# A two-layer decoder trunk: the order of loads and casts in the first pass, and the second mixer's outputs on quarters of the array

## The chip, the cores and the metric

The kernel runs on one core of a Trainium2 chip. Its time is the device time of one execution in microseconds (us). Of the kernel before there are three timed runs, with a median of 755.52 us (754.93 to 756.13), and one profiled execution. PE is the matrix engine, DVE the vector engine, ACT the scalar engine, POOL the GpSimd engine and SP the engine that issues most of the DMAs.

## What is computed

The input is `x`, 256 tokens of width 1024, and one conditioning vector `c`. Each of two layers does

```
mod = silu(c) @ w_ada[i] + b_ada[i]          # six vectors: shift, scale, gate, twice
h = rmsnorm(x, norm_mix[i]) * (1 + sc1) + sh1
x = x + g1 * mixer(h)                        # layer 0: dilated attention; layer 1: gated linear attention
h = rmsnorm(x, norm_ffn[i]) * (1 + sc2) + sh2
x = x + g2 * conv_ffn(h)
```

and the output is `rmsnorm(x, norm_final)`. The second mixer, the gated linear attention, works on chunks of 64 tokens: within a chunk the output is `A @ v` with a masked 64x64 matrix `A` (the part called intra here), and from the chunks before comes `q_t @ s_prev`, with a state of 128x256 per head (the part called inter). Each of its four heads has 128 key and 256 value columns. Its output is normalized per head, multiplied by a gate and projected.

## The kernel before

Activations lie transposed, features on the 128 partitions and the 256 tokens along the free axis, in eight tiles `kt` of 128 features. Most products are done as three passes in the fp32r format: a weight is cast to a high part `whi` by ACT, DVE subtracts that from the weight to get the low part `wlo`, and PE adds hi x hi, hi x lo and lo x hi. The second mixer's products within the chunks are plain fp32 matmuls, each of which shows as two instructions in the trace.

**First pass.** Lines 415 to 470 prepare the eight tiles of the first attention projections. For each `kt`, SP loads one chunk of the modulation weights (1024 KB, called `ada_raw` or `early_x` by the room it lands in) and one chunk of the projection weights (960 KB, `raw`); up to tile 3 each is loaded in two pieces. DVE forms two dot products of the modulation chunk with `silu(c)` (L161), first that of the scale and then that of the shift; ACT adds the bias to each (`mod`, L170 and L172); DVE scales x (`xr`, L432); ACT adds the shift and rounds (`hhi`, L436); DVE makes `hlo` (L440). Beside that ACT casts the weights in two pieces (L448, 768 and 1152 columns) and DVE makes their low parts (L453). The order on ACT is written out by hand: scale's `mod`, first cast, shift's `mod`, `hhi`, second cast; on DVE: two dots, `xr`, first low part, `hlo`, second low part. PE runs the products of a tile (L684 to L690) in a hand-set order, and every tile starts with hi x hi.

Raw weights share four buffers (`raw`), so SP can issue a load only when the DVE has made the low part of an older one, and the odd modulation chunks share one room (`early_x`), free when the dots of the odd tile before are done. SP issues in one queue; where a load's room isn't free, the scheduler may have put a later load ahead of it. Behind the last load SP writes the table of attention biases to DRAM (`rows_d`), from which POOL's own DMA queue fetches the shifted bias tiles (L384 and L385, 16 small transfers for the first two pairs of heads). Behind these POOL loads two more modulation chunks (L495) into the rooms of `early_x` and `x_all`.

**After the first pass.** ACT and DVE take the products out of the PSUM banks (`evacuate`, L597 to L605), which makes room for the next projection, `raw_queries` (L654); the weights of that and of the next values go through the same `raw` buffers, and their casts (L191) are on ACT too.

**Second mixer.** `in_turn` puts groups of products of PE one behind the other. `masked` transposes the decayed keys, forms `A` and copies its causal half into a zeroed tile `a_t` of 128x(2x128) per head, which holds two chunks on its diagonal; `states` forms the states; `outputs` adds the intra part (L1169: 8 matmuls of 128x128 with 128 columns for two heads) and the inter part (L1177: 24 matmuls onto 64 of the output rows with 64 columns) in one PSUM bank for each head; ACT squares each bank, DVE adds, PE sums over features (L1200), and DVE multiplies by the inverse norm (L1210). `key_weights` casts and splits the key and query weights of a head; `decayed` applies the decays (L1104 to L1106).

Of the kernel before, what the change touches and what calls it, by code (L numbers as in the profile page):

```python
# [14 lines left out]
U32 = mybir.dt.uint32  # L15
AF = mybir.ActivationFunctionType
# [41 lines left out]
def trunk(ctx: ExitStack, tc: tile.TileContext, I, out):  # L58
# [37 lines left out]
    def col(at):  # L96
        return small[:, at : at + 1]
# [311 lines left out]

    rooms = [z.rearrange("p k t -> p (k t)")[:, 0:2048] for z in (early_all, x_all)]  # L410

    def load(kt):
        chunk = rooms[0] if kt % 2 else wraw.tile([P, 2048], F32, tag="raw", name="ada_raw")
        for c in (slice(D, 2 * D), slice(0, D)) if kt < 4 else (slice(0, 2 * D),):
            nc.sync.dma_start(chunk[:, c], I["w_ada"][0, kt][:, c])
        raw = wraw.tile([P, 2048], F32, tag="raw", name="raw")
        for c in pieces if kt < 4 else (slice(0, 15 * P),):
            last_load[0] = nc.sync.dma_start(raw[:, c], I["w0"][kt][:, c])
        raw0.append(raw)
        w0.append([wspl.tile([P, 2048], F32R, tag=f"w{part}", name=f"w{part}") for part in ("hi", "lo")])  # L420
        return chunk

    def dots(kt, between=None):
        chunk = load(kt)
# [20 lines left out]
    def cast(kt, half):  # L445
        c = pieces[half]
        with behind(on_act[0]):
            on_act[0] = nc.scalar.copy(w0[kt][0][:, c], raw0[kt][:, c])  # L448
# [4 lines left out]
            on_dve[0] = nc.vector.tensor_tensor(w0[kt][1][:, c], raw0[kt][:, c], w0[kt][0][:, c].bitcast(F32), op=ALU.subtract)  # L453

    def tile_of(kt):
        def first_cast(last):
            on_act[0] = last
            cast(kt, 0)
            return on_act[:1]

        dots(kt, first_cast)
        scaled(kt)
        shifted(kt)
        cast(kt, 1)

    for kt in range(KT):
        tile_of(kt)
# [8 lines left out]
            low(kt, 1)  # L476
    scale_terms(1)
    with tc.issue_after(last_load[0].ins):
        nc.sync.dma_start(rows_d, rows)
        nc.sync.dma_start(small[:, C_CW:], I["small"][:, C_CW:])  # L480

    o_hi, o_lo = [], []
# [219 lines left out]
    for kt in range(1, KT):  # L702
# [4 lines left out]
        for part in (1, 2):  # L707
# [235 lines left out]
    def gt(shape, name, dt=F32, bufs=1, tag=None):  # L943
        return gla.tile(shape, dt, tag=tag or name, name=name, bufs=bufs)
# [125 lines left out]
        with behind(*(run if run[0] else ())):  # L1070
            run[0] = products()

    def key_weights(hd):
        after = ([last_nz], [last_log], last_e)[hd] if hd < 3 else ()
        return split(I["w_qk_b"][hd][:, KT * P :] if hd == 0 else I["w_qk_b"][hd], KT * P if hd == 0 else 2048, after=(after, after))

    def keyed(hd, w, between=None):
        pqk = bank("pqk", "ttpp"[hd])
# [18 lines left out]
    def decayed(hd, pq, pk):  # L1097
        part = min(hd, 1)
        e_q, e_k, e_d, dec = gates[part]
        c = slice(T * (hd - PARTS[part][0]), T * (hd - PARTS[part][0]) + T)  # L1100
        q_t = gt([P, T], "q_t", bufs=4)
        keys = gt([P, 2 * T], "keys", bufs=2)
        k_t, k_d = keys[:, :T], keys[:, T:]
        nc.vector.tensor_tensor(k_d, pk, e_d[:, c], op=ALU.mult)  # L1104
        nc.vector.tensor_tensor(k_t, pk, e_k[:, c], op=ALU.mult)
        nc.vector.scalar_tensor_tensor(q_t, pq, P ** -0.5, e_q[:, c], op0=ALU.mult, op1=ALU.mult)  # L1106
        return q_t, k_t, k_d

    last_st, kv_copy = [None], [None]

    sides = [slice(CH * odd, CH * odd + CH) for odd in range(2)]

    def masked(tag, *two):
        turned, pa = bank("kdt", tag), bank("a", tag)
        kd = gt([P, 2 * T], "kdT", bufs=2)
        a_t = [gt([P, 2, P], "a_t", bufs=4) for _ in two]
        halves = [(i, t, slice(T * i + P * t, T * i + P * t + P)) for i in range(2) for t in range(2)]
        for to in a_t:
            nc.gpsimd.memset(to, 0.0)

        def products():
            for i, t, c in halves:
                last = nc.tensor.transpose(turned[:, c], two[i][2][:, P * t : P * t + P], ident)
            for i, t, c in halves:
                for to in sides:
                    own, at = (slice(z + to.start, z + to.stop) for z in (P * t, c.start))
                    with behind(last):
                        last = mm(pa[to, at], two[i][1][:, own], two[i][0][:, own], start=True, stop=True)
            return last

        in_turn(products)
        nc.scalar.copy(kd, turned)
        for i in range(2):
            for to in sides:
                from_pa = pa[to, T * i : T * i + T].rearrange("p (a b) -> p a b", a=2)[:, :, to]
                nc.vector.copy_predicated(a_t[i][to, :, to], causal[to, :, to].bitcast(U32), from_pa)
        return kd, a_t

    def states(first, kd):
        kv = [bank("kv", tag) for tag in ("s", "s", "t" if first else "s")]  # L1140

        def products():
            for i, n in ((0, 0), (0, 1), (1, 0), (1, 1), (0, 2), (1, 2)):
                t, r = n // 2, slice(CH * (n % 2), CH * (n % 2) + CH)
                last = mm(kv[n][:, T * i : T * i + T], kd[r, T * i + P * t : T * i + P * t + P],
                              v[t][r, T * (first + i) : T * (first + i) + T], start=True, stop=True)
            return last

        in_turn(products)
        st = [gt([P, 2 * T], f"st{n}") for n in range(3)]  # L1150
        kv_copy[0] = nc.scalar.copy(st[0], kv[0])
        for n in (1, 2):
            for i in range(2):
                part = min(first + i, 1)
                at = 4 * (first + i - PARTS[part][0]) + n
                c = slice(T * i, T * i + T)
                last_st[0] = nc.vector.scalar_tensor_tensor(st[n][:, c], st[n - 1][:, c], gates[part][3][:, at : at + 1], kv[n][:, c],
                                                            op0=ALU.mult, op1=ALU.add)
        return st

    def outputs(first, two, a_t, st):
        po = [bank("o", "s") for _ in range(2)]

        def products():
            for i in range(2):
                for et in range(2):
                    ev = slice(T * (first + i) + P * et, T * (first + i) + P * et + P)
                    for t in range(2):
                        mm(po[i][:, T * et + P * t : T * et + P * t + P], v[t][:, ev], a_t[i][:, t, :],  # L1169
                           start=(et == t == 0), stop=False)  # L1170
            for i in range(2):
                for et in range(2):
                    for n in range(1, 4):
                        c = slice(CH * n, CH * n + CH)
                        for to in sides:
                            at = T * i + P * et + to.start
                            last = mm(po[i][to, T * et + CH * n : T * et + CH * n + CH], st[n - 1][:, at : at + CH], two[i][0][:, c],  # L1177
                                      start=False, stop=(et == 1 and n == 3))
            return last

        in_turn(products)
        sq = gt([P, 4 * T], "osq", tag="D1").rearrange("p (i e t) -> p i e t", i=2, e=2)
        for i in range(2):
            nc.scalar.activation(sq[:, i, :, :], po[i].rearrange("p (e t) -> p e t", e=2), AF.Square)
        acc = gt([P, 2 * T], "oacc", tag="keys", bufs=2).rearrange("p (i t) -> p i t", i=2)
        nc.vector.tensor_tensor(acc, sq[:, :, 0, :], sq[:, :, 1, :], op=ALU.add)
        return po, acc

    o_n = []
# [1 line left out]
    def normed_outputs(first, po, acc):  # L1191
# [15 lines left out]
        for i in range(2):  # L1207
            on = gt([P, 2 * T], "on", tag=f"st{i}" if first else f"on{i}").rearrange("p (e t) -> p e t", e=2)
            for et in range(2):
                last_on = nc.vector.scalar_tensor_tensor(on[:, et, :], po[i][:, T * et : T * et + T], col(C_GN + et), rr[:, T * i : T * i + T],  # L1210
                                               op0=ALU.mult, op1=ALU.mult)
            o_n.append(on)
        return last_on

    r_g = []
# [278 lines left out]
```

## Time and profile before

| what | value |
|---|---|
| median of three runs | 755.52 us |
| the profiled execution, its own time | 754.74 us |
| its span | 753.0 us |
| PE busy | 745.0 us |
| DVE busy | 630.5 us |
| ACT busy | 491.5 us |
| DMA moved | 186.83 MB, mean 248 GB/s |
| granted PE clock | 1.0 |

The span is what the profile covers; the execution's own time is 1.74 us longer. A line number (L453) is that of the kernel before. Times in the rows below are us from the start of the span. "Idle before" an instruction is time in which its engine had nothing to do, and the arrow names what ended it. A row with x4 stands for four merged instructions.

### The profile page before, as it was taken

What the parts mean: (1) busy time and instruction counts of PE and PEld (TensorE: products, weight loads), DVE (VectorE), ACT (ScalarE), POOL (GpSimd) and SP (SyncE); (2) the same over time, 40 slices, a digit from 0 to 9 for tenths busy, and PEclk for the clock granted to TensorE, in tenths of its full rate; (3) what the DMA queues carried; (4) which work ended last, traced back from release to release, by engine and by line L of the source; (5) the groups of instructions that cost most, each with busy time, mean ns of one, the idle gap of its engine ahead of it and who ended that gap; (6) DMA issues with size and microseconds to landing.
All of it is one profiled execution on the core that took longest, in us unless ns stands there. A gap on an engine that the chain in (4) does not pass through costs nothing.

```text
span 753.0 us, 16106 instructions
## 1 busy us (share of the span) xinstructions
PE 745.0 (99%) x6474; PEld 723.7 (96%) x6474; DVE 630.5 (84%) x1124; ACT 491.5 (65%) x954; POOL 78.2 (10%) x148
## 2 busy tenths in 40 slices
PE   9999999999999999999999999999999999999997
PEld 7999999999999999999999998899999999999996
DVE  7988977887978688999988778987897989898672
ACT  6467676576666588676766547845878766666552
POOL 6243320320200010000000002000010000000100
PEclk9999999999999999999999999999999999999999
DMA  8999788888886666866646985873475755556741
GB/s 340 417 353 369 246 297 308 292 280 280 288 282 227 235 224 220 285 225 229 241 147 229 329 315 180 340 277 130 155 279 172 277 188 204 198 181 216 266 149 56
DMA packets 31997, 186.83 MB, mean 248 GB/s; under 512 B 4386, under 2 KB 4770, under 8 KB 16051
## 3 DMA queue, kind: packets, MB, share of 16 engines
q1 hardware_dynamic: 26816, 162.38, 60.0%
q0 software_dynamic: 4784, 23.09, 9.4%
q8 instruction: 50, 0.82, 0.4%
q10 hardware_dynamic: 322, 0.35, 0.1%
q14 instruction: 25, 0.20, 0.1%
HBM read 184.70 MB, written 1.10 MB: 247 GB/s over the span
## 4 chain that ended last, share of the span: by engine, by line
PE 88%; DVE 5%; DMA 3%; ACT 2%; issue 1%; SPq 0%; ACTq 0%; DVEq 0%
PE pab L216 10%; PE pab L217 10%; PE pab L218 10%; PE pd L216 5%; PE pd L217 5%; PE pd L218 5%; PE pqk L216 5%; PE pqk L217 4%; PE pqk L218 4%; PE pv L217 3%; PE pv L218 3%; PE pv L216 3%; DMA early_x<-in_w_ada 2%; PE py L217 2%; PE py L218 2%; PE py L216 2%
## 5 line engine op out<-in xcount | busy, mean ns | idle before, releaser
L195 DVE TENSOR_TENSOR wlo<-raw,whi 128x1024 fp32r<-128x1024 f32 (+3 forms) x254 | 272.4, 1105 | 54.7 <-ACT whi L191 53.6
L191 ACT CAST whi<-raw 128x1024 fp32r<-128x1024 f32 (+3 forms) x254 | 228.6, 949 | 107.4 <-PE pab L217 40.8
L218 PE MATMUL pab<-hhi,wlo 128*128 128x256 f32 x672 | 184.9, 276 | 0.0
L217 PE MATMUL pab<-hlo,whi 128*128 128x256 f32 x672 | 184.8, 277 | 0.0
L216 PE MATMUL pab<-hhi,whi 128*128 128x256 f32 x672 | 183.4, 277 | 0.0
L218 PEld LDWEIGHTS pab<-hhi,wlo 128*128 128x128 f32 x672 | 126.2, 188 | 0.0
L217 PEld LDWEIGHTS pab<-hlo,whi 128*128 128x128 f32 x672 | 126.0, 188 | 0.2
L216 PEld LDWEIGHTS pab<-hhi,whi 128*128 128x128 f32 x672 | 125.2, 188 | 0.1
L217 PE MATMUL pd<-glo,whi 128*128 128x256 f32 x352 | 97.1, 276 | 0.0
L218 PE MATMUL pd<-ghi,wlo 128*128 128x256 f32 x352 | 97.1, 276 | 0.0
L216 PE MATMUL pd<-ghi,whi 128*128 128x256 f32 x352 | 96.8, 276 | 0.0
L216 PE MATMUL pqk<-hhi,whi 128*128 128x256 f32 x314 | 88.2, 281 | 0.0
L217 PE MATMUL pqk<-hlo,whi 128*128 128x256 f32 x314 | 87.0, 277 | 0.0
L218 PE MATMUL pqk<-hhi,wlo 128*128 128x256 f32 x314 | 87.0, 277 | 0.0
L161 DVE CUSTOM_DVE_ANT_0 ada_raw<-ada_raw,c_bc 128x1024 f32<-128x1024 f32 x52 | 61.4, 1222 | 8.2 <-DMA ada_raw<-in_w_ada 8.2
L217 PEld LDWEIGHTS pd<-glo,whi 128*128 128x128 f32 x352 | 66.1, 188 | 0.0
L218 PEld LDWEIGHTS pd<-ghi,wlo 128*128 128x128 f32 x352 | 66.1, 188 | 0.0
L216 PEld LDWEIGHTS pd<-ghi,whi 128*128 128x128 f32 x352 | 65.9, 188 | 0.0
L216 PEld LDWEIGHTS pqk<-hhi,whi 128*128 128x128 f32 x314 | 59.1, 188 | 0.5
L217 PEld LDWEIGHTS pqk<-hlo,whi 128*128 128x128 f32 x314 | 59.0, 188 | 0.0
L218 PEld LDWEIGHTS pqk<-hhi,wlo 128*128 128x128 f32 x314 | 59.0, 188 | 0.0
L897 ACT ACTIVATE r<-pab,small 128x256 f32<-128x256 f32 x86 | 46.8, 561 | 15.7 <-DVE r L900 15.6
(244 smaller groups left out, 1500.8 us busy)
## 6 DMA issues: line engine op xcount, KB each, us to landing
raw<-in_w_up SPq DMA_DIRECT2D x42, 1024.0 KB, 4.8
ada_raw<-in_w_ada SPq DMA_DIRECT2D x24, 1024.0 KB, 5.0
raw<-in_w_down SPq DMA_DIRECT2D x32, 704.0 KB, 5.1
raw<-in_wqk SPq DMA_DIRECT2D x18, 1024.0 KB, 5.8
raw<-in_wv SPq DMA_DIRECT2D x14, 768.0 KB, 6.3
early_x<-in_w_ada POOLq DMA_DIRECT2D x9, 1024.0 KB, 6.6
x_all<-in_w_ada POOLq DMA_DIRECT2D x9, 1024.0 KB, 6.2
raw<-in_w_out_a SPq DMA_DIRECT2D x4, 1024.0 KB, 5.3
```

The source lines that it names most:

```text
L161: last_dot[0] = nc.vector.tensor_tensor_reduce(w, w, c_bc, op0=ALU.mult, op1=ALU.add, scale=1.0, scalar=0.0, accum_out=dot,)
L191: copied[0] = nc.scalar.copy(hi[:, c], raw[:, c])
L195: last_lo[0] = nc.vector.tensor_tensor(lo[:, c], raw[:, c], hi[:, c].bitcast(F32), op=ALU.subtract)
L216: mm(ps, a[0], b[0], start=start, stop=False)
L217: mm(ps, a[0], b[1], start=False, stop=False)
L218: return mm(ps, a[1], b[0], start=False, stop=stop)
L897: nc.scalar.activation(r, u[:, :T], AF.Identity, scale=cw[2], bias=col(C_CB + 44 * l + f))
```

## The change

In the first pass every load is queued on SP behind the one before it, in the order modulation chunk, projection chunk, tile by tile, and the write of `rows_d` goes behind the loads of tile 5 and not behind all loads. From tile 3 on, the first cast stands ahead of both `mod`s on ACT and the second cast between them, so both stand ahead of `hhi`. The casts of the first weights after the pass are queued behind the last `hhi` (`after=on_act`).

In the second mixer, the low parts of the last head's key weights are queued on DVE behind `q_t` of the second head. `a_t` loses its empty halves. The intra part becomes 32 matmuls of 64x64 with 64 columns: the first and second chunk of a token half lie on the upper and lower 64 partitions and go to two PSUM banks, so that a bank now holds the even or odd chunks of both heads, and no longer all chunks of one head. The inter part has its 24 matmuls as before, to the new places. The squares and the normalization read the banks in the new order, 64 columns at a time; two heads' states 0 and 1 share one tile, as do two heads' outputs.

```diff
+    def in_turn(to, of):
+        with behind(*(last_load if last_load[0] else ())):
+            last_load[0] = nc.sync.dma_start(to, of)
     def load(kt):
...
-            nc.sync.dma_start(chunk[:, c], I["w_ada"][0, kt][:, c])
+            in_turn(chunk[:, c], I["w_ada"][0, kt][:, c])
...
-            last_load[0] = nc.sync.dma_start(raw[:, c], I["w0"][kt][:, c])
+            in_turn(raw[:, c], I["w0"][kt][:, c])
+        if kt == 5:
+            in_turn(rows_d, rows)
...
     def tile_of(kt):
-        def first_cast(last):
+        def one_cast(last):
             on_act[0] = last
+            cast(kt, int(kt > 2))
+            return on_act[:1]
+
+        chunk = load(kt)
+        if kt > 2:
             cast(kt, 0)
-            return on_act[:1]
-
-        dots(kt, first_cast)
+        dots(kt, chunk, one_cast)
         scaled(kt)
         shifted(kt)
-        cast(kt, 1)
+        if kt < 3:
+            cast(kt, 1)
...
     with tc.issue_after(last_load[0].ins):
-        nc.sync.dma_start(rows_d, rows)
         nc.sync.dma_start(small[:, C_CW:], I["small"][:, C_CW:])
...
-    pq, pk, middle, end = raw_queries(2, 0, tag="t", low=left[2][1:], by_parts=True)
+    pq, pk, middle, end = raw_queries(2, 0, tag="t", low=left[2][1:], by_parts=True, after=on_act)
...
-                        mm(po[i][:, T * et + P * t : T * et + P * t + P], v[t][:, ev], a_t[i][:, t, :],
-                           start=(et == t == 0), stop=False)
...
+            for i, et, t in np.ndindex(2, 2, 2):
+                at = T * et + P * i
+                for q, own in enumerate(sides):
+                    for to in sides:
+                        ev = T * (first + i) + P * et + to.start
+                        mm(po[q][to, at + CH * t : at + CH * t + CH], v[t][own, ev : ev + CH], a_t[i][own, t, :],
+                           start=(i == et == t == 0), stop=False)
...
-    w = key_weights(3)
+    w = key_weights(3, last_q)
```

## Rows read from the trace of the kernel before

**Rows 1.** The page: busy time, share of the span and instructions per engine.
```profile
PE 745.0 (99%) x6474; PEld 723.7 (96%) x6474; DVE 630.5 (84%) x1124; ACT 491.5 (65%) x954; POOL 78.2 (10%) x148
```
**Rows 2.** PE's waits: engine, line, releaser, us in total, times, longest.
```profile
PE kdt L1123 <- DVE keys L1104: 0.2, 1, 0.2
```
**Rows 3.** The chain of waits: start us, us, engine and line.
```profile
28.22 9.61 DMA early_x<-in_w_ada
...
64.91 0.62 PE s L524 x32
...
515.22 1.78 PE o L1169 x16
517.00 1.55 PE o L1177 x48
...
532.95 0.46 PE ms L1200 x2
```
**Rows 4.** DVE in time, tiles 5 to 7: start us, us, line, operation.
```profile
37.85 1.23 DVE L161 CUSTOM_DVE_ANT_0 early_x<-early_x,c_bc 128x1024 f32<-128x1024 f32 x1 [0.48 <-DMA early_x<-in_w_ada]
...
43.59 1.22 DVE L161 CUSTOM_DVE_ANT_0 ada_raw<-ada_raw,c_bc 128x1024 f32<-128x1024 f32 x1
...
48.05 1.36 DVE L453 TENSOR_TENSOR wlo<-raw,whi 128x1152 fp32r<-128x1152 f32 x1 [0.42 <-ACT whi L448]
49.33 1.22 DVE L161 CUSTOM_DVE_ANT_0 early_x<-early_x,c_bc 128x1024 f32<-128x1024 f32 x1
```
**Rows 5.** ACT in time, tile 6.
```profile
44.85 0.39 ACT L170 ACTIVATE mod<-dot,one_b,small 128x1 f32<-128x1 f32 x1 [2.57 <-DVE dot L161]
45.15 0.83 ACT L448 CAST whi<-raw 128x768 fp32r<-128x768 f32 x1
...
46.45 0.51 ACT L436 ACTIVATE hhi<-xr,mod 128x256 fp32r<-128x256 f32 x1 [0.16 <-DVE xr L432]
46.87 1.15 ACT L448 CAST whi<-raw 128x1152 fp32r<-128x1152 f32 x1
```
**Rows 6.** PE in time: tile 2 begins, tile 3 begins, first work after the pass.
```profile
24.10 1.52 PE L690 MATMUL pqk<-hhi,whi 128*128 128x256 f32 x12
...
29.26 2.02 PE L690 MATMUL pqk<-hhi,whi 128*128 128x256 f32 x12
...
58.40 1.98 PE L654 MATMUL pqk<-hhi,whi 128*128 128x256 f32 x16
```
**Rows 7.** SP's queue in time; x2 are the issues of two loads.
```profile
22.48 3.78 SPq L418 DMA_DIRECT2D raw<-in_w  x2
...
33.95 3.77 SPq L418 DMA_DIRECT2D raw<-in_w  x2
37.78 0.42 SPq L479 DMA_DIRECT2D rows_d<-rows  x1
```
**Rows 8.** The load issued at 22.48: KB, us from issue to landing.
```profile
raw<-in_w SPq DMA_DIRECT2D x1, 960.0 KB, 10.5
```
**Rows 9.** The same of the load issued at 33.95.
```profile
raw<-in_w SPq DMA_DIRECT2D x1, 960.0 KB, 9.0
```
**Rows 10.** DMA queues, 40 to 47 us (SP's is q1): packets, MB, share of 16 engines.
```profile
q1 hardware_dynamic: 556, 2.90, 101.9%
```
**Rows 11.** DMA queues, 49 to 55 us (POOL's is q0).
```profile
q1 hardware_dynamic: 228, 1.23, 70.3%
q0 software_dynamic: 261, 0.42, 29.7%
```
**Rows 12.** POOL in time: first bias transfer, first chunk into a room.
```profile
45.78 0.69 POOL L384 DMA_DIRECT2D bias<-rows_d  x1 [21.62 <-DMA rows_d<-rows]
...
58.44 0.57 POOL L495 DMA_DIRECT2D early_x<-in_w_ada  x1 [0.50 <-DVE k L598]
```
**Rows 13.** ACT after the pass: casts of the next weights, first evacuation.
```profile
53.66 3.47 ACT L191 CAST whi<-raw 128x1024 fp32r<-128x1024 f32 x4
57.02 0.65 ACT L597 ACTIVATE q<-pqk 128x256 f32<-128x256 f32 x2
```
**Rows 14.** DVE in time: what the second sum of squares waits for.
```profile
530.56 0.69 DVE L1196 TENSOR_TENSOR osq<-oacc,osq 128x512 fp32r<-128x512 f32 x1 [0.69 <-ACT osq L1195]
```

More of the change, by code (lines that the diff above doesn't have):

```diff
@@ L421, in load, with dots @@
         return chunk
-    def dots(kt, between=None):
-        chunk = load(kt)
+    def dots(kt, chunk, between):
         with behind(on_dve[0], on_act[0]):
@@ L1071, in in_turn, with key_weights @@
             run[0] = products()
-    def key_weights(hd):
+    def key_weights(hd, low=()):
         after = ([last_nz], [last_log], last_e)[hd] if hd < 3 else ()
-        return split(I["w_qk_b"][hd][:, KT * P :] if hd == 0 else I["w_qk_b"][hd], KT * P if hd == 0 else 2048, after=(after, after))
+        return split(I["w_qk_b"][hd][:, KT * P :] if hd == 0 else I["w_qk_b"][hd], KT * P if hd == 0 else 2048, after=(after, after), low=low, late=low)
     def keyed(hd, w, between=None):
@@ L1105, in decayed @@
         nc.vector.tensor_tensor(k_t, pk, e_k[:, c], op=ALU.mult)
-        nc.vector.scalar_tensor_tensor(q_t, pq, P ** -0.5, e_q[:, c], op0=ALU.mult, op1=ALU.mult)
+        last_q[0] = nc.vector.scalar_tensor_tensor(q_t, pq, P ** -0.5, e_q[:, c], op0=ALU.mult, op1=ALU.mult)
         return q_t, k_t, k_d
-    last_st, kv_copy = [None], [None]
+    last_st, kv_copy, last_q = [None], [None], [None]
     sides = [slice(CH * odd, CH * odd + CH) for odd in range(2)]
@@ L1115, in masked @@
         kd = gt([P, 2 * T], "kdT", bufs=2)
-        a_t = [gt([P, 2, P], "a_t", bufs=4) for _ in two]
+        a_t = [gt([P, 2, CH], "a_t", bufs=4) for _ in two]
         halves = [(i, t, slice(T * i + P * t, T * i + P * t + P)) for i in range(2) for t in range(2)]
@@ L1135, in masked @@
                 from_pa = pa[to, T * i : T * i + T].rearrange("p (a b) -> p a b", a=2)[:, :, to]
-                nc.vector.copy_predicated(a_t[i][to, :, to], causal[to, :, to].bitcast(U32), from_pa)
+                nc.vector.copy_predicated(a_t[i][to, :, :], causal[to, :, to].bitcast(U32), from_pa)
         return kd, a_t
@@ L1149, in states @@
         in_turn(products)
-        st = [gt([P, 2 * T], f"st{n}") for n in range(3)]
+        st = gt([P, 4 * T], "st")
+        st = [st[:, : 2 * T], st[:, 2 * T :], gt([P, 2 * T], "st2")]
         kv_copy[0] = nc.scalar.copy(st[0], kv[0])
@@ L1164, in products @@
         def products():
[L1165 to L1168, printed above, removed]
-                        mm(po[i][:, T * et + P * t : T * et + P * t + P], v[t][:, ev], a_t[i][:, t, :],
-                           start=(et == t == 0), stop=False)
[L1171 to L1178, printed above, removed]
+            for i, et, t in np.ndindex(2, 2, 2):
[5 more added lines that the diff above has]
+                           start=(i == et == t == 0), stop=False)
@@ L1179, in products @@
+            for i, et in np.ndindex(2, 2):
+                of = T * i + P * et
+                for n in range(1, 4):
+                    at = T * et + P * i + CH * (n // 2)
+                    for to in sides:
+                        last = mm(po[n % 2][to, at : at + CH], st[n - 1][:, of + to.start : of + to.stop], two[i][0][:, CH * n : CH * n + CH],
+                                  start=False, stop=(i == et == 1 and n > 1))
             return last
         in_turn(products)
-        sq = gt([P, 4 * T], "osq", tag="D1").rearrange("p (i e t) -> p i e t", i=2, e=2)
@@ L1183, in outputs @@
-        for i in range(2):
-            nc.scalar.activation(sq[:, i, :, :], po[i].rearrange("p (e t) -> p e t", e=2), AF.Square)
+        sq = gt([P, 4 * T], "osq", tag="D1")
+        for q in range(2):
+            nc.scalar.activation(sq.rearrange("p (b q c) -> p b q c", q=2, c=CH)[:, :, q, :], po[q].rearrange("p (b c) -> p b c", c=CH), AF.Square)
+        sq = sq.rearrange("p (e i t) -> p e i t", i=2, e=2)
         acc = gt([P, 2 * T], "oacc", tag="keys", bufs=2).rearrange("p (i t) -> p i t", i=2)
-        nc.vector.tensor_tensor(acc, sq[:, :, 0, :], sq[:, :, 1, :], op=ALU.add)
+        nc.vector.tensor_tensor(acc, sq[:, 0, :, :], sq[:, 1, :, :], op=ALU.add)
@@ L1206, in normed_outputs @@
         norm_ops[1] = nc.scalar.activation(rr, ln, AF.Exp, scale=-0.5)
[L1207 to L1212, printed above, removed]
+        on = gt([P, 4 * T], "on", tag="st" if first else "on")
+        own = on.rearrange("p (e b q c) -> p e b q c", e=2, q=2, c=CH)
+        by = rr.rearrange("p (b q c) -> p b q c", q=2, c=CH)
+        for et, q in np.ndindex(2, 2):
+            last_on = nc.vector.scalar_tensor_tensor(own[:, et, :, q, :], po[q][:, T * et : T * et + T].rearrange("p (b c) -> p b c", c=CH),
+                                                     col(C_GN + et), by[:, :, q, :], op0=ALU.mult, op1=ALU.mult)
+        o_n.extend(on.rearrange("p (e i t) -> p i e t", i=2, e=2)[:, i] for i in range(2))
         return last_on
```

## The prediction

> **What bounds the kernel now.** The page comes first: PE is busy 745.0 of 753.0 us [rows 1], so nothing shortens the kernel but less work on PE or fewer of its gaps. PE's waits come second. Of those, the one in the second mixer that the change touches is 0.2 us for the keys [rows 2]. The chain of waits comes third. Until 58 us it runs through DVE, ACT and DMAs, with one piece of 9.61 us that is the modulation chunk of tile 5 on its way [rows 3]. So the first pass is bound by what feeds PE, and the second mixer by PE itself. A us saved at either place shortens the kernel by as much, since PE then works on without a gap, as long as what follows isn't late for another reason.
>
> The first pass in detail: DVE takes 5.74 us for a tile (from 43.59 to 49.33), and 0.42 of that is a wait for ACT's second cast [rows 4], because that cast stands behind `hhi` [rows 5]. Tile 5 waited 0.48 us more for its chunk [rows 4], whose load was issued at 28.22, behind a projection chunk that had gone ahead of it [rows 3, 7]. PE's own work for a tile is 5.16 us (24.10 to 29.26) [rows 6], so DVE is the slower of the two by little.
>
> **The first pass, step by step.** Both casts ahead of `hhi` take the 0.42 us out: a tile costs DVE 5.32 us. But the cast that now stands first on ACT needs the projection chunk, and `mod`, `xr` and `hhi` queue behind it. From the landing of that chunk to the end of `hhi` it takes the first cast 0.83, a `mod` 0.30, the second cast 1.05 (1.15 less the overlap of neighbours), a `mod` 0.30 and `hhi` 0.45: 2.9 us [rows 5].
>
> Tile 4's chunk lands at 22.48 + 10.5 = 33.0 [rows 7, 8], so its `hhi` ends at 35.9, and `hlo` (0.4) and the second low part (1.3) end at 37.6. In the trace DVE was through with tile 4 at 37.4, 0.48 before 37.85 [rows 4]. So tiles 3 and 4 gain nothing; the new wait for the chunk replaces the old one. Then come the gains. In turn, tile 5's modulation chunk is next on the queue and lands some 2.5 us after 33.0 (1.05 MB at 0.41 MB per us [rows 10]), so that DVE begins tile 5 at 37.6, tile 6 at 42.9 and tile 7 at 48.2, where it began at 49.33 [rows 4]. `hhi` of tile 7 ends 3.35 later (43.59 to 46.96 in tile 6 [rows 4, 5]), at 51.6, and PE needs 5.16 from there: the pass ends at 56.7, not 58.4 [rows 6]. Gain 1.7 us, if the last projection chunk is in time. For this it has to land before 51.6 - 2.9 = 48.7.
>
> Does it? The chunk of tile 6 lands at 33.95 + 9.0 = 42.95 [rows 7, 9] with the same loads ahead of it in both orders. Behind it come 2.03 MB (tile 7's two chunks), 4.9 us at 0.41 MB per us [rows 10], with the 48 KB of `rows_d` some 48.0. That is 0.7 us to spare, and now the moved write counts. It was issued at 37.78 [rows 7] and is now issued right behind the loads of tile 5, near 28.9. It lands behind that tile's chunk (33.0 + 4.9, say 38.0), and POOL, which waits for nothing else [rows 12], begins the 16 bias transfers at 38.3 in place of 45.78. Their packets showed from 49 us on, over 3 us after the first issue. Moved by 7.5 us they flow from 41.7 and meet the loads of tile 7, where they met loads that weren't urgent. The price from both sides: nothing, if they find room; 3.0 us by the bytes of SP's queue (1.23 MB in 6 us where 2.48 would have gone); 1.8 us by the time that POOL's packets themselves took (29.7% of 6 us) [rows 10, 11]. I take 1.8, since that is engine time which the loads can't have, while part of the lost bytes may be SP's queue running thin. Then the last chunk lands at 49.8, `hhi` ends at 52.7, and the pass at 57.9. Gain 0.5 us; by the ends, a gain of 1.7 or a loss of 0.7.
>
> **The second mixer.** The intra part is 16 instructions in 1.78 us for two heads, twice in the kernel [rows 3]. It becomes 64 instructions on quarters. The nearest row is the attention's own 64x64 products: 32 instructions with 64 columns in 0.62 us, 19.4 ns each [rows 3]. 64 of these are 1.24 us, a gain of 0.54, twice 1.08. The ends: four at a time at the pace of the old instruction (111 ns for 128 columns, 56 for 64) give 0.89 us, a gain of 0.89; the pace of the inter part, 1.55 us for 48 [rows 3], gives 2.07, a loss of 0.29. The inter part keeps count and shape: 0.
>
> Low parts behind `q_t`: the keys come earlier and the 0.2 us of [rows 2] go; the low parts are then wanted only by the fourth head's products, after the third head's and the states: 0. The squares of a bank now wait for the end of both heads, and DVE's reads go in steps of 64 columns, element for element the same. What hides that: DVE has the second sum's input ready at 531.25, and PE takes it at 532.95 [rows 3, 14], 1.7 us later. PE comes 1.1 earlier, so 0.6 are left, and more than that would appear in full. Smaller `a_t`: POOL's time, 0.
>
> **Sum.** -0.5 - 1.08 - 0.2 = -1.8 us. The profiled execution took 754.74 us, so 752.9; it lies 0.78 below the median of the runs, so 753.7.
>
> **Rivals.** *The bias transfers cost the bytes (3.0 us).* The pass ends at 59.1, 0.7 late; with the mixer's 1.3 the sum is -0.6: 754.9. For it speaks that SP's queue moved only half its bytes in that stretch [rows 11]. The Trainium skill ("DMA: Bandwidth & Descriptors", Queues, rings and completion order) says that each DMA engine goes round between the queues that have work, packet by packet; the two shares in [rows 11] agree, and by that rule a late load gets no precedence over the bias.
>
> *ACT is held by a cast whose weight isn't there: slower.* Behind the bias transfers POOL loads two chunks of 1.05 MB into the rooms, at 58.44 [rows 12]. POOL is now through some 7 us earlier, and the first room is free when tile 7's dots end, at 50.5, so these 2.1 MB flow from 52 on, 5.1 us of all engines [rows 10]. They meet the weights of the next projection and of the next values. In the trace the casts of both stand on ACT ahead of the first evacuation [rows 13], without which PE has no bank for its next products. After 49.8 SP's queue still has 2.02 MB up to the values' first half, 4.9 us: 54.7 alone, 59.8 behind the two chunks. Casts of 1.7 and an evacuation of 0.8 [rows 13] put PE at 62.3, 4.4 late: 758.1. It decides from the point at which that half lands after 55.4. Against it: the scheduler may put the evacuation first, or POOL's loads may get only a share.
>
> *Everything finds room.* The pass ends at 56.7 and the quarters run four at a time: -1.7 - 0.2 - 1.08 to 1.78, between 751.8 and 752.5.
>
> *Quarters bring nothing.* If each instruction costs its issue and not its columns, 64 take as long as 16 did: -0.7, 754.8. Against it: 19.4 ns for each [rows 3]. The Trainium skill ("TensorEngine Tiling (Array Packing)", Instruction Overhead) gives a matmul about 60 cycles whatever its columns and warns against cutting a dimension that is already small; at 2.4 GHz an estimate from it is 25 ns x 64 = 1.6 us, a gain of 0.2 for each call.
>
> **How the numbers follow.** Forecast 0.32 (its own range 752.9 to 754.5, of which a quarter is under 0.2%), everything finds room 0.22, bias by bytes 0.20, ACT held 0.20, quarters nothing 0.06. A change of 0.2%, 1.5 us, is about what a measurement here can tell from none. Faster: 0.22 + 0.24 = 0.46. Same: 0.08 + 0.17 + 0.06 = 0.31. Slower: 0.20 + 0.03 = 0.23. The range goes from the better end, 751.8, to 757.6, which leaves out most of the held case.
>
> **What would show it.** Right: DVE's wait for the cast gone from tile 4 on, and in its place ACT waits for `raw`; the first bias transfer near 38; `hhi` of tile 7 near 52.7 and the first product after the pass near 57.9; 64 instructions of the intra part in 1.24 us; no wait of PE for the keys. Wrong: a PE wait of some us between 56 and 63 (held); tile 7's `hhi` at 51.6 or before (bias free) or after 53.5 (bias by bytes); the intra part at 1.6 us or more; or a gap of PE at the second sum of squares.

## The result and the profile after

The changed kernel takes 759.15 us (757.76 to 759.94), the kernel before in the same session 755.52: ratio 1.0052, interval 1.0038 to 1.0066. So it is slower by 3.6 us, and the forecast was a gain of 1.8. The profiled execution took 759.69, its span is 757.9.

The page of the changed kernel, busy time, to be held against [rows 1]:

```profile
PE 744.6 (98%) x6570; PEld 723.5 (95%) x6570; DVE 631.0 (83%) x1124; ACT 489.5 (65%) x954; POOL 76.7 (10%) x148
```

PE is busy for 0.4 us less, though the span is 4.9 us longer. What the mixer saves, 0.69 us twice, is hidden here by matmuls that ran at a lower clock, by estimate 1.4 us (below). The rest is new gaps, and PE's waits in the changed kernel name them (engine, line, releaser, us in total, times, longest):

```profile
PE pqk L698 <- ACT hhi L441: 3.8, 4, 2.5
PE pqk L216 <- ACT v L623: 2.1, 1, 2.1
...
PE pqk L662 <- DVE wlo L195: 0.7, 1, 0.7
```

The wait for the keys [rows 2] is gone, as forecast. New are 2.5 us in the first pass, 0.7 right behind it and 2.1 at the copies of the first values. Line numbers are those of the changed kernel from here on: L453 is the first pass's cast, L441 its `hhi`, L662 the first products after the pass, L605 the first evacuation.

PE in time: tile 7 begins, the first work after the pass (58.40 in [rows 6]), the products that wait for the copies, and two of the matmuls behind them.

```profile
54.10 1.68 PE L698 MATMUL pqk<-hhi,whi 128*128 128x256 f32 x12 [2.47 <-ACT hhi L441]
...
59.48 1.98 PE L662 MATMUL pqk<-hhi,whi 128*128 128x256 f32 x16
...
80.58 0.58 PE L216 MATMUL pqk<-hhi,whi 128*128 128x256 f32 x1 [2.14 <-ACT v L623]
...
81.17 0.41 PE L218 MATMUL pqk<-hhi,wlo 128*128 128x256 f32 x1
81.39 0.41 PE L216 MATMUL pqk<-hhi,whi 128*128 128x256 f32 x1
```

Around the third of these, by 2 us (us, PE busy, instructions, granted clock, DMA share, GB/s):

```profile
76.00:78.00 2.00, 2.00 (x34) 1.00 1.08 363
78.00:80.00 2.00, 0.45 (x32) 1.00 0.93 319
80.00:82.00 2.00, 1.42 (x6) 0.55 1.03 397
82.00:84.00 2.00, 2.00 (x13) 0.60 1.02 410
84.00:86.00 2.00, 2.00 (x20) 1.00 0.96 406
```

PE stood idle for 2.14 us, and then the granted clock was 0.55 to 0.60 for some 3 us, the level of 1.2 GHz: matmuls begin 0.21 us apart (81.17, 81.39) where they begin 0.115 apart at 84.0. By estimate, 14 matmuls at 0.1 us more each, that is 1.4 us on top of the gap.

ACT on tile 7: the cast waits 5.00 us for the projection chunk, and everything up to `hhi` queues behind it. After the pass a cast of the values' weights waits 1.30 us more, with the second evacuation behind it.

```profile
51.15 0.83 ACT L453 CAST whi<-raw 128x768 fp32r<-128x768 f32 x1 [5.00 <-DMA raw<-in_w]
51.89 0.38 ACT L170 ACTIVATE mod<-dot,one_b,small 128x1 f32<-128x1 f32 x1
...
53.55 0.51 ACT L441 ACTIVATE hhi<-xr,mod 128x256 fp32r<-128x256 f32 x1
...
59.60 1.57 ACT L191 CAST whi<-raw 128x768 fp32r<-128x768 f32 x2 [1.30 <-DMA raw<-in_wv]
61.08 0.38 ACT L605 ACTIVATE q<-pqk 128x256 f32<-128x256 f32 x1
```

POOL, first bias transfer and the two chunks into the rooms (45.78 and 58.44 in [rows 12]):

```profile
37.73 0.69 POOL L384 DMA_DIRECT2D bias<-rows_d  x1 [14.67 <-DMA rows_d<-rows]
...
51.21 0.57 POOL L503 DMA_DIRECT2D early_x<-in_w_ada  x1 [0.27 <-DMA bias<-rows_d]
53.09 0.54 POOL L503 DMA_DIRECT2D x_all<-in_w_ada  x1 [1.31 <-DVE xr L437]
```

DVE's dots of tiles 5, 6 and 7 follow each other without the wait of [rows 4]; then `xr` waits for ACT:

```profile
37.08 1.22 DVE L161 CUSTOM_DVE_ANT_0 early_x<-early_x,c_bc 128x1024 f32<-128x1024 f32 x1
...
42.30 1.21 DVE L161 CUSTOM_DVE_ANT_0 ada_raw<-ada_raw,c_bc 128x1024 f32<-128x1024 f32 x1
...
47.85 1.22 DVE L161 CUSTOM_DVE_ANT_0 early_x<-early_x,c_bc 128x1024 f32<-128x1024 f32 x1
...
52.31 0.48 DVE L437 SCALAR_TENSOR_TENSOR xr<-x_all,mod,rstd 128x256 f32<-128x256 f32 x1 [2.08 <-ACT mod L170]
```

The chain in the second mixer, against the x16 and x48 of [rows 3]:

```profile
520.80 1.09 PE o L1179 x64
521.89 1.55 PE o L1186 x48
...
537.29 0.46 PE ms L1210 x2
```

So the loss is laid down by 94 us: PE is 1.08 us later than before at the end of the pass, 6.46 later at the first outputs of the attention (94.41 against 87.95), and gets back 1.5 by the end, nearly all of it in the mixer. These first outputs, in the changed kernel and then in the one before:

```profile
94.41 1.08 PE L585 MATMUL po<-pt,v 128*64 128x256 f32 x8
```

```profile
87.95 1.08 PE L577 MATMUL po<-pt,v 128*64 128x256 f32 x8
```

### The profile page after: what moved, and what is told of

It reads as the page before. It is cut to its first block, busy times and chain, and to the rows that moved or that the text cites. A ratio compares the mean times of both kernels' runs of the same rounds, so it can differ in the third digit from the quotient of the medians.

```text
span 757.9 us, 16298 instructions
## 1 busy us (share of the span) xinstructions
PE 744.6 (98%) x6570; PEld 723.5 (95%) x6570; DVE 631.0 (83%) x1124; ACT 489.5 (65%) x954; POOL 76.7 (10%) x148
## 4 chain that ended last, share of the span: by engine, by line
PE 87%; DMA 6%; DVE 3%; ACT 2%; issue 1%; SPq 0%; ACTq 0%
PE pab L218 10%; PE pab L217 10%; PE pab L216 10%; PE pd L216 5%; PE pd L218 5%; PE pqk L216 5%; PE pd L217 5%; PE pqk L218 5%; PE pqk L217 5%; PE pv L217 3%; PE pv L218 3%; PE pv L216 3%; DMA raw<-in_w 3%; PE py L217 2%; PE py L218 2%; PE py L216 2%
```

## Experiments

Each was timed against the kernel before on the same chip. "Pass end" is the start of PE's first product after the first pass, "gap" PE's wait for the copies of v near 78 us, both from the one profiled execution of each kernel. The medians of the kernel before moved by 0.9 us from session to session, so where two kernels of different sessions lie close, the text also gives their distances from the kernel before of their own session.

| kernel | median us | ratio, interval | pass end | gap |
|---|---|---|---|---|
| before | 754.7 to 755.5 | 1 | 58.40 | 0 |
| changed | 759.15 | 1.0052 (1.0038 to 1.0066) | 59.48 | 2.14 |
| e1 write late | 751.32 | 0.9953 (0.994 to 0.9965) | 56.75 | 0 |
| e2 mixer alone | 752.82 | 0.9972 (0.9962 to 0.9982) | 58.29 | 0 |
| e3 first pass alone | 760.59 | 1.0072 (1.0058 to 1.0087) | 59.75 | 2.1 |
| e4 early write alone | 760.43 | 1.0071 (1.0054 to 1.0087) | 61.31 | 0 |
| e5 bias held, new tile | 757.71 | 1.0057 (1.003 to 1.0084) | 56.48 | 0 |
| e6 rooms held, new tile | 766.09 | 1.0143 (1.0107 to 1.018) | 61.55 | 1.82 |
| e7 mods behind copies | 757.88 | 1.0032 (1.002 to 1.0043) | 60.26 | 1.09 |
| e8 evacuations first | 758.89 | 1.0047 (1.0034 to 1.006) | 61.22 | 2.07 |
| e9 bias held | 751.74 | 0.9952 (0.9938 to 0.9965) | 57.23 | 0 |
| e10 rooms held | 758.83 | 1.0055 (1.004 to 1.0069) | 59.75 | 1.71 |
| e11 dots behind | 760.54 | 1.007 (1.0056 to 1.0083) | 60.85 | 2.07 |
| e12 casts alone | 752.62 | 0.9967 (0.9955 to 0.9979) | 57.91 | 0.62 |
| e13 copies first | 756.68 | 1.0031 (1.0019 to 1.0043) | 61.02 | 0 |
| e14 write behind tile 6 | 753.69 | 0.9991 (0.9982 to 1.0) | 58.40 | 0.30 |
| e15 load order alone | 756.83 | 1.0025 (1.0014 to 1.0035) | 58.25 | 2.81 |

**e1, the write of `rows_d` back behind all loads, all else as changed.**

```diff
-        if kt == 5:
-            in_turn(rows_d, rows)
...
+        nc.sync.dma_start(rows_d, rows)
         nc.sync.dma_start(small[:, C_CW:], I["small"][:, C_CW:])
```

> The changed kernel, with the write of rows_d back behind the last load of the first pass; all else as changed. Theory T (traffic: the bias transfers and the two room chunks, started earlier by the moved write, delay tile 7's weights and the weights after the pass): the last projection chunk lands near 48, hhi of tile 7 ends near 51.6, the first product after the pass starts near 57, no PE gap near 78, and the time is 1.7 + 1.6 us below before: 752 to 754 us. Theory O (the strict order of loads, or the casts ahead, costs the time): PE still waits 2 us or more for hhi of tile 7, and the time stays at 757 us or more. Theory S (the move made the scheduler write another order of ACT's and DVE's work after the pass, and that order stalls PE, not the traffic): the gap near 78 goes, but tile 7's wait of 2.5 us stays, 755 to 756 us.

751.32, faster than both kernels, and 7.8 us under the changed one (7.05 by the sessions' own kernels before). Tile 7's chunk lands 3.5 us earlier, at 47.65, and PE has no gap from 40 to 100 us. ACT, PE and POOL of this kernel in time:

```profile
47.65 0.84 ACT L453 CAST whi<-raw 128x768 fp32r<-128x768 f32 x1 [1.61 <-DMA raw<-in_w]
...
50.75 0.51 ACT L441 ACTIVATE hhi<-xr,mod 128x256 fp32r<-128x256 f32 x1
```

```profile
56.75 1.98 PE L662 MATMUL pqk<-hhi,whi 128*128 128x256 f32 x16
```

```profile
48.04 0.69 POOL L384 DMA_DIRECT2D bias<-rows_d  x1 [24.02 <-DMA rows_d<-rows]
```

The DMA queues from 41 to 51 us say why (packets, MB, share of 16 engines; SP's is q1, POOL's q0), the changed kernel first, then e1:

```profile
q1 hardware_dynamic: 479, 2.57, 84.3%
q0 software_dynamic: 304, 0.47, 17.3%
```

```profile
q1 hardware_dynamic: 720, 3.96, 96.7%
```

The early bias moved 0.47 MB in these 10 us and SP's loads moved 1.39 MB less. At the 0.41 MB per us of [rows 10] that is 3.4 us, what the last chunk came late (3.5).

**e2, the mixer's part alone; e3, the first pass's part alone** (with the early write). Each takes one part of the change into the kernel before.

```diff
+    w = key_weights(3, last_q)            # e2: with the change's other edits of the mixer
...
+            in_turn(raw[:, c], I["w0"][kt][:, c])   # e3: with its other edits of the first pass
+        if kt == 5:
+            in_turn(rows_d, rows)
```

> The kernel before with the second mixer's part of the change alone (intra products on quarters, banks by chunk, low parts of the last key weights behind q_t). The intra part takes 1.09 us in place of 1.78, twice, and the 0.2 us wait for the keys goes: 1.6 us less, 753.9 us. If later stages give that back: 755.5 us.

> The kernel before with the first pass's part of the change alone. If the two parts add up, it is slower than the whole change by the mixer's 1.6 us: 760.7 us, 5 us above before, and PE is 6.4 us late from 95 us on. If the loss came from the two together, it lies near 755 us.

The mixer brings 1.9 us (752.82), and the first pass with the early write costs 5.8 (760.59). Both parts add up to about what the whole change does (+3.9, measured +3.6), so nothing of the loss comes from the mixer.

**e4, the early write alone, in the kernel before.**

```diff
             last_load[0] = nc.sync.dma_start(raw[:, c], I["w0"][kt][:, c])
+        if kt == 5:
+            with behind(last_load[0]): nc.sync.dma_start(rows_d, rows)
...
-        nc.sync.dma_start(rows_d, rows)
```

> The kernel before with one edit: rows_d is written behind the loads of tile 5. Theory T: the bias transfers begin near 37 us and take 3 us from tile 7's two loads; the last of them lands near 51.5 in place of 48.5, the pass ends 1.5 to 3 us later, and the time is 758 to 761 us. Theory O: no change, 755.5 us. Theory S: the pass ends near 58.4 as before, PE has a gap of some 2 us near 75 us, 757 to 759 us.

760.43: this one line alone costs the kernel before 5.7 us. POOL's first bias transfer comes at 35.22, and the pass ends at 61.31, 2.9 us late; at the attention's first outputs it is still 2.9 (90.87 against 87.95). This profiled execution is the fastest of the six, 757.72 us at a mean granted clock of 0.999. The others took 759.79 to 762.33 at 0.995 to 0.997, so the rest of the 5.7 us shows in no profile.

**e5 and e9, the early write kept, its bias transfers held.** POOL copies one column of tile 7's projection chunk before the first bias transfer, so that the transfers wait until that chunk has landed. e5 puts the column into a new tile of 4 bytes a partition (three buffers), e9 into one that the kernel has already. Both have the same order on every engine.

```diff
+    hold = nc.gpsimd.tensor_copy(tmp.tile([P, 1], F32, tag="hold", name="hold"), raw0[7][:, 0:1])  # e5
+    hold = nc.gpsimd.tensor_copy(tmp.tile([P, 1], F32, tag="dot", name="hold", bufs=4), raw0[7][:, 0:1])  # e9
-    bias = load_bias(0)
+    with behind(hold): bias = load_bias(0)
```

> The changed kernel with the early write of rows_d, but POOL is held before its 16 bias transfers by a copy of one column of tile 7's projection chunk, so that it begins them when that chunk has landed. Theory T (the cost of the early write is that POOL's transfers begin 10 us earlier and meet the loads that feed PE): first bias transfer near 48 as with the late write, the pass ends near 57, about 752 us (751 to 753). Rival W (the write itself, or its place on SP's queue, costs): the time stays above 756, with the last projection chunk landing near 51. The order of ACT and DVE behind the pass comes out like that with the late write here too, so this run does not part T from the rival S (another order of ACT).

> As the kernel with the bias transfers held until tile 7's chunk has landed, with the same order on every engine, but the held copy writes into a tile that the kernel has already, so that no later tile has another place in SBUF. That run had its first pass whole (no wait of PE for hhi over 0.2 us, pass end 56.5) and was yet at 757.7 with matmuls of the gated layers at 281 ns where the others show 276. Theory P (the extra tile of 4 bytes a partition moved the later tiles, and PE reads them slower): 276 ns again and 751 to 753 us, so theory T (the early write costs by the transfers that it lets go early) stands. Rival: 281 ns and 757 to 758 again: then the cost is not the place of the tiles, and an early write costs something that the first pass does not show.

e5 came to 757.71 (756.33 to 765.59 in twelve runs; the profiled one took 760.24), though its pass ended at 56.48 and its gap was gone. The time was lost elsewhere: in the gated layers PE had no gap, and yet did 1022 matmuls in 120 us where e9 did 1060. The two windows, each followed by one group of its matmuls (busy us, mean ns), e5 first:

```profile
580.00:700.00 120.00, 120.00 (x1022) 1.00 0.58 198
```

```profile
L218 PE MATMUL pab<-hhi,wlo 128*128 128x256 f32 x300 | 84.3, 281 | 0.0
```

```profile
580.00:700.00 120.00, 120.00 (x1060) 1.00 0.60 206
```

```profile
L218 PE MATMUL pab<-hhi,wlo 128*128 128x256 f32 x296 | 81.7, 276 | 0.0
```

With the old tile e9 takes 751.74, all but the 751.32 of e1. So the early write is harmless in itself; it costs through the transfers that it lets go, and holding these alone takes 7.4 us off the changed kernel (7.2 by the sessions' own kernels before). e9 also brings back e1's order on ACT behind the pass, so this run doesn't divide the 7.4 between late data and order.

**e6 and e10, only POOL's two room chunks held,** behind a copy from the first evacuation; e10 has the copy in an existing tile. Every engine keeps the changed kernel's order.

```diff
+    hold = nc.gpsimd.tensor_copy(..., qk0[0][1][:, 0:1])
-    with behind(last_bias[0]):
+    with behind(last_bias[0], hold):
```

> The changed kernel; only POOL's two chunks into the rooms are held, by a copy that reads q[1] of the first evacuation, so they begin near 58.5 instead of 51.2 and 53.1. Every engine has the same order as in the changed kernel. Theory T: the bias still delays tile 7 (last hhi near 53.5, pass end near 58), but the weights behind the pass land in time: the 1.2 us lost between 58 and 64 go, and if the gap near 78 is a consequence of late weights it goes too: 755 to 756. Rival S (the order of ACT makes the gap): only the 1.2 us go, and the gap near 78 and the low clock stay: about 758.

> As the kernel with only the two room chunks held behind the first evacuation, with the held copy in a tile that the kernel has already. Order on every engine as in the changed kernel, matmuls of the gated layers at 276 ns if theory P holds. Then: if the room chunks are what delays the weights behind the pass, the values' cast no longer waits 1.3 us and PE not 0.7 for low parts: 757.5 to 758.5. The gap near 78 stays (it showed 1.8 us with the rooms held), so not under 757. Rival (the weights are late by the pass itself): 759 to 760.

e6 has the slow matmuls of e5 (281 ns) and says nothing more. e10: 758.83, no gain that can be told from the changed kernel. In its profile, of its fastest run (756.19), the cast no longer waits for the values' weights and PE not for their low parts, but the gap stays (1.71). The room chunks are a small part of it.

**e7, e11 and e13, the gap near 78.** PE waits for the copies of the first values. In the changed kernel they stand on ACT behind two `mod`s that wait for DVE's dots and behind two exponentials; in e1 they come earlier:

```profile
74.81 0.29 ACT L172 ACTIVATE mod<-dot,small 128x1 f32<-128x1 f32 x1 [4.66 <-DVE dot L161]
...
77.10 0.61 ACT L559 ACTIVATE prob<-prob,m 128x384 f32<-128x384 f32 x1
...
79.24 0.36 ACT L620 COPY v<-pv 64x256 f32<-64x256 f32 x1
```

```profile
70.50 0.62 ACT L559 ACTIVATE prob<-prob,m 128x384 f32<-128x384 f32 x1 [0.18 <-DVE m L556]
...
71.93 0.37 ACT L620 COPY v<-pv 64x256 f32<-64x256 f32 x1
...
74.44 0.48 ACT L172 ACTIVATE mod<-dot,small 128x1 f32<-128x1 f32 x2
```

e7 puts the `mod`s behind the copies, e11 the dots too behind the first probabilities, e13 the copies ahead of `mod`s and exponentials. Transfers stay as changed.

```diff
-    with behind(last_max[0]):
-        room_ada()
     v = by_groups(pv)
-    before = probabilities(*raised)
+    with behind(last_max[0], last_v[0]):  # e13
+        room_ada(); before = probabilities(*raised)
```

> The changed kernel with one difference of order: the two mods of the first chunk from a room stand on ACT behind the copies of the first values, where the changed kernel has them ahead of two casts, two exponentials and these copies. Transfers as in the changed kernel. Rival S: the gap of 2.1 us near 78 and the low clock behind it go or shrink, some 2 to 3.6 us less than the changed kernel, 755.5 to 757. Theory T (late transfers make the gap whatever the order): within 0.7 us of the changed kernel, 758.5 to 760.

> The changed kernel with the first chunk from a room used later: its two dots on DVE behind the first probabilities and its two mods on ACT behind the copies of the first values. The transfers start as in the changed kernel. Theory S (the early chunk made the scheduler put dots ahead of the maxima's sign change, on which exponentials and behind them the copies of the values wait; the run with the mods alone moved took 1.1 of the 2.1 us): no wait of PE for a copy of v near 78, clock 1.0 throughout, 755.3 to 756.5. Rival: the copies are late because the values' weights were late; then over 757.5.

> The changed kernel with the copies of the first values on ACT ahead of the two mods of the first room chunk and of the first exponentials, where the changed kernel has them behind both. PE, POOL and SP keep the changed kernel's order. Theory S2 (the gap of 2.1 us near 78 and the low clock behind it come from the copies' place on ACT, behind exponentials that wait for DVE): no PE wait for a copy of v over 0.3 us, clock 1.0 from 78 to 84, 3 to 3.6 us less than the changed kernel: 755.5 to 756.5. What is left above the kernel with the late write (751.3) is then the pass and what follows it at once. Rival: the copies wait for the last values' products anyway, and PE runs into the same wait: 758.5 or more.

e7 took half the gap and 1.3 us (0.7 by the sessions' own kernels before), which isn't clear of the noise. e11 missed: the exponentials still stood ahead of the copies, waiting 4.73 us for DVE, the gap was 2.07, and at 760.54 nothing was gained. e13 took the gap: the copy follows its products at once, the clock is 1.0 from 60 to 92 us, and it takes 756.68, 2.5 under the changed kernel (1.6 by the sessions' own kernels before). So the gap is the order of ACT, not data that comes late; PE, POOL and SP keep the changed kernel's order, and DVE's shifts a little with ACT's.

```profile
76.88 0.37 ACT L620 COPY v<-pv 64x256 f32<-64x256 f32 x1 [2.09 <-PE pv L218]
```

e13's profile also shows what the wait for tile 7 can cost beyond itself. Up to 57 us eight kernels (the changed one, e3, e6, e7, e8, e10, e11, e13) have the same order on PE, ACT, DVE and SP, and in all of them PE waits 1.86 to 2.71 us for tile 7. In four the clock stayed at 1.00 from 52 to 60 us and the pass ended at 59.48 to 60.26; in e6, e8, e11 and e13 it fell behind the wait, and the pass ended at 60.85 to 61.55. So the changed kernel's profile shows the cheaper case. Tile 7's first products in e13, to be held against 1.68 us at 54.10:

```profile
54.28 2.93 PE L698 MATMUL pqk<-hhi,whi 128*128 128x256 f32 x12 [2.56 <-ACT hhi L441]
```

The order near 78 is the scheduler's: nothing in the change names it. It wrote one order with the write behind tile 5 and another with the write behind all loads.

**e8, casts of the next values' weights behind all evacuations.**

```diff
-        values(1, 0, pv, low=left[-1][1:])
+        values(1, 0, pv, after=left[-1][:1], low=left[-1][1:])
```

> The changed kernel with the casts of the first half of the next values' weights behind the evacuations on ACT, where the changed kernel has them behind the first evacuation only. It tests the prediction's rival that ACT is held by a cast whose weight is late. If so: the second evacuation no longer waits 1.3 us for that weight, PE loses up to 1.2 us less between 58 and 64, about 758. If PE there waits for the low parts of the same weights anyway: no change, 759.2, or a little worse, as the casts come later.

758.89, not to be told from 759.15. In its profile the wait for low parts is gone, and from the pass end to the scores PE takes 5.75 us (61.22 to 66.97), 1.0 less than in the changed kernel (59.48 to 66.22). But its pass ended later, with a granted clock of 0.59 from 56 to 60 us. So the held cast costs PE about 1 us, and that doesn't show in the median.

**e14, the write behind tile 6.**

```diff
-        if kt == 5:
+        if kt == 6:
             in_turn(rows_d, rows)
```

> The changed kernel with the write of rows_d behind tile 6's loads instead of tile 5's: a dose between the changed kernel and the late write. The first bias transfer comes near 43 instead of 37.7 or 48.0. Theory T (what counts is how many of the bias transfers flow while tile 7's loads are on their way): tile 7's chunk lands between 47.7 and 51.1, some 49 to 50, pass end 57 to 58.5, 752 to 756. Rival (any early write costs the same): 758 or more; (the bias harms only tile 7's first chunk): 751.5.

753.69, between the two. Bias transfers begin at 42.99; tile 7's cast still starts at 47.90, as in e1. But POOL reaches the room chunks at 56.86, and now ACT holds the first evacuations behind a cast of the values' weights; ACT, then PE:

```profile
56.04 1.56 ACT L191 CAST whi<-raw 128x768 fp32r<-128x768 f32 x2 [0.94 <-DMA raw<-in_wv]
```

```profile
58.40 2.10 PE L662 MATMUL pqk<-hhi,whi 128*128 128x256 f32 x16 [1.62 <-DVE k L606]
```

**e12 and e15, e1 taken apart:** casts ahead without the load order, load order without the casts (late write and mixer's part in both).

```diff
-        with behind(*(last_load if last_load[0] else ())):
+        if True:  # e12
...
-            cast(kt, int(kt > 2))
+            cast(kt, int(kt > 7))  # e15, and so with the two other tests of kt
```

> The kernel with the late write of rows_d (751.3) without the strict order of the loads: casts ahead of scale and shift, the mixer's part, but projection chunks may again go ahead of modulation chunks. Two theories of the first pass's gain of some 1.6 us: C (the casts' order takes 0.4 us off every tile from 5 on, three tiles, and the load order only the 0.48 us that tile 5 waits): about 751.8. L (casts ahead of hhi gain only if the chunks come in turn, since the cast now waits for the projection chunk and mod, xr and hhi queue behind it): 753 or more, no better than the mixer's part alone (752.8).

> The kernel with the late write of rows_d (751.3) with the casts back in the old places (first cast between the mods, second behind hhi): strict load order and the mixer's part alone. With casts alone 752.6 was measured, no better than the mixer's part alone (752.8). Theory B (both are needed: the load order brings tile 5's chunk in time, the casts take the 0.42 us wait off each tile): 752.3 to 752.8 here too. Theory O (the order of the loads does it alone, the casts nothing): 751.3 to 751.7.

Neither brings what both do, though e12's 1.3 us above e1 (0.8 by the sessions' own kernels before) aren't clear of the noise. In e12 SP also issued the write at 38.32 again, ahead of tile 7's modulation chunk. Its PE is ready for the next products at 57.52 (57.91 less a wait of 0.39), 0.9 before the kernel before; its time is that of e2. In e15 the pass ends at 58.25, as before, and PE then waits 2.81 us for copies that stand behind four exponentials on ACT, with a granted clock down to 0.50 (80 to 82 us) after it. There late data is part of it: the cast ahead of the exponentials waits 5.59 us for its weight. So 756.83 holds a gap like that of the changed kernel and not the price of the load order. What the load order would bring without that gap wasn't measured.

```profile
72.43 2.00 ACT L191 CAST whi<-raw 128x1024 fp32r<-128x1024 f32 x2 [5.59 <-DMA raw<-in_wqk]
```

```profile
78.25 0.39 PE L216 MATMUL pqk<-hhi,whi 128*128 128x256 f32 x1 [2.81 <-ACT v L623]
```

## Why the prediction was wrong

**Two steps failed: the price of the moved bias transfers, and a term that the sum doesn't have, for what follows the first pass.** In the profile the pass ended at 59.48 where 57.9 was forecast, 1.6 us. From there to the attention's first outputs PE lost 5.4 us more against the kernel before (1.08 late, then 6.46), which the sum put at nothing.

**The price.** The prediction bounded it by 0 and 3.0 us and took 1.8, the engine time that POOL's own packets had taken [rows 11], "since that is engine time which the loads can't have". The runs show 3.5 us (chunk landed at 51.15 against 47.65), past the upper end. The loads lost more than the engine time of the bias: q1 had 84.3% of the engines in the changed kernel and 96.7% in e1, but moved 2.57 MB against 3.96, so its own packets took a third longer beside the bias (32.8 against 24.4 share points per MB). The count by bytes, which the prediction kept as a rival at 3.0, was the right one; with the bytes of this stretch it gives 3.4. The Trainium skill ("DMA: Bandwidth & Descriptors", Queues, rings and completion order) lets each engine go round between queues by packet. The counts don't speak against it (304 of 783 packets were the bias's), but from the share of packets or of time alone the loss of bytes couldn't be read.

**The chance of the slower rival was too low, and its price was right for another reason.** "ACT is held by a cast whose weight isn't there" had 0.20 at 758.1. It happened: the second evacuation stood behind a cast that waited 1.30 us, PE for low parts 0.7, and PE's lag behind e1 grew from 2.7 at the end of the pass to 3.9 at the scores (66.22 against 62.28), not 4.4 more. e8 shows about 1 us of it, e14 the same mechanism without the late tile 7, 1.62 us.

**No step named the gap near 78.** 2.14 us of it and 1.4 us of low clock are as large as the whole loss. A us saved in the pass was to count in full "as long as what follows isn't late for another reason"; apart from the held cast the prediction named no such reason, and took the order of ACT and DVE behind the pass as fixed. The moved write alone changed both (the changed kernel against e1). e13 shows that the copies' place is worth 1.6 to 2.5 us in the median.

Against e1, in the profiles: 2.7 up to the end of the pass, 1.2 more up to the scores, 2.1 and 1.4 at the copies make 7.4 of the 8.1 us at the attention's first outputs (94.41 against 86.31). Of the remaining 0.7 most lies between the scores and the copies, 0.28 of it a wait for low parts at 72.82; the cause of the rest, and of 0.9 later on, stays open.

**What came as written.** The bias began at 37.73 (38.3 forecast). DVE's wait for the cast went, and its dots began at 37.08, 42.30 and 47.85, tiles 5.2 to 5.6 us apart (5.32). Without the bias the pass ends at 56.75 (e1), where the prediction had 56.7. This part is worth some 1.5 us (752.82 of e2 to 751.32 of e1). The pass ended at 57.91 with the casts alone (e12) and at 58.25 with the load order alone (e15), so by these profiles it needs both; in the median e15's gap hides what the load order is worth. There was no wait for the keys, and no gap at the second sum of squares. One slip had no effect: from tile 6's first dot to the end of its `hhi` the rows give 3.37 us, not 3.35.

**The mixer was mis-sized to the good side.** 64 instructions took 1.09 us, 17 ns each, where the attention's row gave 19.4, so each call gained 0.69 and not 0.54; with the keys that is 1.6 of the 1.9 us that e2 measures. "Quarters bring nothing" is refuted by that. The Trainium skill ("TensorEngine Tiling (Array Packing)", Instruction Overhead) gives a matmul about 60 cycles, by estimate 25 ns at 2.4 GHz. Here, with 64x64 blocks in turn on the four quarters, an instruction took 17 ns, and a matmul of the kernel, which is two of them, 34.

## What to carry to other kernels

A small transfer that many others wait for is a valve: before its place on a queue is moved, ask which transfers it lets go, what is on its way then, and price them by the bytes that the other queue loses, not by their own. The scheduler answered an earlier transfer with another order on engines that the edit doesn't touch, so compare the orders as well as the waits. Here the best kernel is the change without that move: 751.32 us, 0.9953 (0.994 to 0.9965) of the kernel before.

## What the hardware showed unexpectedly

- After PE had stood idle the granted clock sometimes fell and sometimes not. Near 78 us it was 0.55 to 0.60 after 2.14 us in the changed kernel; after 2.07 us it was 0.62 from 80 to 84 in e11 and 1.00 in e8; after 1.82 us it was 0.74 in e6, after 1.71 us 1.00 in e10. In the pass, 2.47 us were followed by 1.00 in the changed kernel and by 0.83 (52 to 56 us) and 0.75 (56 to 60) in e6. What decides between these stays open.
- With one more tile of 4 bytes a partition, that nothing reads, the gated layers' matmuls were slower: 1022 against 1060 in 120 us at the same order on every engine and a granted clock of 1.00 (e5, e9), 757.71 against 751.74 us, and the runs lay 9.3 us apart where e9's lay 0.9; in the other pair (e6, e10) it was 766.09 against 758.83. That the tile moves the places of later tiles in SBUF is the likely cause, but not shown: no run moved single tiles.
- Loads of a large-packet queue took a third more engine time per MB while a small-packet queue was at work beside them (see above).
